# Stick-breaking attention with its heads cut into stages, projection blocks set between the stages in a fixed TensorE order, and the rotary tables computed during the first MLP

## Chip, core and metric

The kernel runs on one core of a Trainium2 chip. The metric is the device time of one execution in microseconds (us), as the median of several runs. Engine names in the profile: PE is TensorE (matmul), PEld its weight load, DVE is VectorE, ACT is ScalarE, POOL is GpSimd, SP is the engine that issues most DMAs.

## What is computed

Two transformer blocks over 512 tokens of width 1024, all in float32. The part that the change touches is the first half of block 1 and one small table of block 2:

```
h    = rmsnorm(x, g_pre_mix);  proj = h @ w_in           # pool input, q, k, v
z    = q @ k.T * scale                                   # 8 heads of 64, strictly causal
attn = where(mask, exp(log_sigmoid(z) + tail), 0)        # tail: sum of log(1-sigmoid(z)) to the right
o_sb = attn @ v
gates = sigmoid(h @ w_gate + b_gate)
merged = gates[:, :1024]*y_pool + gates[:, 1024:]*y_sb
x = x + rmsnorm(merged @ w_out);  x = x + rmsnorm(relu(..w_up)^2 @ w_down)   # block 1's MLP
cos, sin = rope_tables(positions)                        # used by the two layers of block 2
```

## The kernel before

Activations lie with features on partitions and the 512 tokens along the free axis. Every float32 product is made of three matmuls of rounded parts (`mm3`, L373 to L375): weight-high by activation-high and by activation-low, weight-low by activation-high. A projection of 128 output features (`proj`) is 8 such blocks, 24 matmuls of 512 columns. The weights come as units of 8 blocks in a fixed list (`weight_plan`); `prep` (L344 to L354) loads a unit by a DMA of SP, rounds it on ACT (`whi`, L352) and takes the rest on POOL (`wlo`, L353), three units ahead of use, with four buffers for each of the two parts.

Block 1 begins with the norm's split of x and its sum of squares, the values of all heads (96 matmuls), then `r`, the reciprocal root of the norm (`rsqrt`, L459 to L461 on DVE). Then follow q and k of the first pair of heads, a transposition of r to a column (`column`, eight small matmuls at L487 that read r), and the values' eviction with that column. `rope_tables` (L808 to L859) is called next: about 25 DVE instructions of 128x512 on tiles of the pool `xp`, a sine and four copies on ACT, one DMA of the positions.

The loop over four pairs of heads projects q and k of the next pair (`qk`), then runs `head` twice. A head has four handovers between TensorE and the two vector engines. TensorE writes the scores into three PSUM banks zC, zB, zA (12 matmuls, L577 to L579). For each bank ACT takes Abs (L584), Exp and Ln (L337), DVE a maximum and sum (L587), ACT the rounded part (L590), DVE the rest (L591). TensorE adds the sums to the right into the banks in the order zC, zB, zA (L597, L602). ACT takes Exp of each bank (L337) and the rounded part (L610), DVE the rest (L611), and TensorE multiplies by the values (8 matmuls, L615). Behind the two heads of a pair stand the projections of some gates (`EARLY`) and one of the pooled branch (`pool`). With the first pair the stage has 22 projections; 20 of them come behind the column.

Nobody writes down the order of the instructions: the program's calls are in this order, and a scheduler arranges each engine's queue by its own estimate of times, so that TensorE's queue mixes projections and steps of the heads. Each engine then runs its queue in order; a waiting instruction holds all behind it. PSUM has three banks `mm` for projections, one `av`, one `st` and the three of the scores.

Of the kernel before, what the change touches and what calls it, by code (L numbers as in the profile page):

```python
# [35 lines left out]
EARLY = ((), (0,), (1, 2), (3, 4))  # L36
# [20 lines left out]
LAG = 5  # L57
WHOLE = (slice(0, S),)
# [188 lines left out]
class Kern:  # L247
# [93 lines left out]

# [58 lines left out]
    def proj_halves(self, pool, tag, acts, n, done, finish):  # L400
        """The last n columns of outputs, by halves of the tokens: done(column, its half, tokens),
        and finish(tokens) after the last column of a half, behind the first products of the next."""
        w = [[self.take(ahead=AHEAD if j == 0 and k < UNIT else 2) for k in range(len(acts))] for j in range(n)]
        ready = None
        for cs in HALVES:
            for j in range(n):
                ps = pool.tile([P, S // 2], F32, name=tag)
                for k, a in enumerate(acts):
                    self.mm3(ps, w[j][k], [t[:, cs] for t in a], k == 0, k == len(acts) - 1)
                    if k == LAG and ready is not None:  # L410
                        finish(ready)
                        ready = None
                done(j, ps, cs)
            ready = cs
        finish(ready)

# [1 line left out]
    def split(self, pool, src, tags, scale=None, lo_eng=None):  # L418
        """src (times a per-partition scale) as two float32r parts."""
        hi, lo = (pool.tile([P, S], FR, name=t) for t in tags)  # L420
        self.split_into(hi, lo, src, scale, lo_eng)
        return hi, lo

    def split_into(self, hi, lo, src, scale=None, lo_eng=None):
        nc = self.nc
        if scale is None:
            nc.scalar.copy(out=hi, in_=src)  # L427
            (lo_eng or nc.vector).tensor_tensor(out=lo, in0=src, in1=hi.bitcast(F32), op=ALU.subtract)
# [5 lines left out]
    def sq_add(self, acc, src, first, eng=None):  # L434
        """acc += src^2."""
# [16 lines left out]
    def rsqrt(self, out, src, n):  # L452
        """out = (src / n + eps)^-1/2: exp(-ln / 2), and a Newton step on it."""
# [9 lines left out]
    def norm_in(self, pool, gname, l, produce=None, parts=WHOLE, on_pool=KT - 2):  # L463
        """The split of x*g, tile by tile, and what gives r = rsqrt(mean(x^2) + eps)."""
# [18 lines left out]
    def column(self, pool, pp, tag, row):  # L483
        """[128, 512] with equal partitions -> [128 tokens, 4 token tiles]."""
# [8 lines left out]
    def block1(self):  # L493
# [12 lines left out]
        atp = at.__enter__()  # L506
        pp_ = tc.tile_pool(name="pp1", bufs=1, space=PSUM, reuse_waits="tile")
# [10 lines left out]
        # constants of the stick-breaking attention  # L518
# [17 lines left out]
        # v, with tokens on partitions  # L536
# [9 lines left out]
        def qk(p):  # L546
            res = []
            q = self.proj(ppw, "mm", acts)
# [11 lines left out]
            k = self.proj(ppw, "mm", acts)  # L560
# [7 lines left out]
            return res  # L568
# [4 lines left out]
        def head(h, kk, qh, ql, o):  # L573
# [19 lines left out]
            for j in (3, 2, 1, 0):  # L593
# [9 lines left out]
            av = ptile("av")  # L603
            at_ = {}
            for b, n in (("zA", S), ("zB", 384), ("zC", S)):
                t = self.xp.tile([P, S], F32, name="x")[:, :n]
# [5 lines left out]
                at_[b] = (hi, lo)  # L612
            for j, (b, c0, q0, n) in enumerate(where):
                for i, part in enumerate(at_[b]):
                    mm(av[:, q0:S], lhsT=vst[j][:, h, :], rhs=part[:, c0 : c0 + n], start=j == 0 and i == 0, stop=j == 3 and i == 1)  # L615
# [6 lines left out]
        def pool(g):  # L622
            """Trailing means of window w minus the token itself."""
            w = WINDOWS[g]
            ps = self.proj(ppw, "mm", acts)
# [3 lines left out]
            while step < w:  # L629
                s2 = self.xp.tile([P, S], F32, name="x")  # L630
# [8 lines left out]
        heads = qk(0)  # L639
        rcol = self.column(atp, ppw, "st", r)  # L640
        vst = []
        for t in range(4):
            vt = atp.tile([P, SBH, P], FR, name="v", bufs=4)
            src = vps[t].rearrange("p (h d) -> p h d", d=SBD)
            A.activation(out=vt[:, :, 0:SBD], in_=src, func=AF.Identity, scale=rcol[:, t : t + 1], bias=0.0)
            V.scalar_tensor_tensor(out=vt[:, :, SBD:P], in0=src, scalar=rcol[:, t : t + 1], in1=vt[:, :, 0:SBD].bitcast(F32), op0=ALU.mult, op1=ALU.subtract)
            vst.append(vt)
        self.rope_tables()
        for p in range(4):
            now, heads = heads, qk(p + 1) if p < 3 else None  # L650
            o = atp.tile([P, S], F32, name="o", bufs=1)
            for e in range(2):
                head(2 * p + e, *now[e], o)
            oacts.append(self.split(brp, o, ("oh", "ol")))
            for i in EARLY[p]:
                for half in range(2):
                    ps = self.proj(ppw, "mm", acts)
# [16 lines left out]
        # pooled branch  # L674
# [7 lines left out]
        # gates and merge  # L682
# [25 lines left out]
        # output projection, norm, residual  # L708
# [33 lines left out]
        # MLP  # L742
# [5 lines left out]
        for c in range(nch):  # L748
            a = []
            pss = self.proj_outer(pp, "b", acts, FIRST1, HALVES) if c == 0 else []  # L750
            for f_ in range(CHUNK1):
# [4 lines left out]
                a.append(self.split(fp, ps, ("ah", "al")))  # L756
            if c < nch - 1:
# [50 lines left out]
    def rope_tables(self):  # L808
# [7 lines left out]
        t = lambda n: self.xp.tile([P, S], F32, name="x")  # L816
        pi = self.xp.tile([P, S], I32, name="x")
        nc.sync.dma_start(out=pi, in_=self.pos_d.broadcast_to((P, S)))
        a, d, hi, lo = t("ta"), t("td"), t("thi"), t("tlo")
# [9 lines left out]
        V.tensor_copy(out=a, in_=pi)  # L829
# [32 lines left out]
    def layer2(self, l, produce=None, after=None):  # L862
# [16 lines left out]
        # gated input of the convolution  # L879
# [20 lines left out]
        # shared rotary part of the keys  # L900
# [12 lines left out]
        # low-rank inputs of keys, values and queries  # L913
# [138 lines left out]
        # convolution: tile 0 and some taps of tile 3 off VectorE, the others on it  # L1052
# [47 lines left out]
        # layer norm over the convolution's channels, silu  # L1100
# [32 lines left out]
        # MLP  # L1133
# [38 lines left out]
    def final(self, pp, a):  # L1172
        """The last columns of the last layer, the norm, the output."""
# [62 lines left out]
```

## Time and profile before

| | |
|---|---|
| median of 3 runs | 1931.41 us (1929.58 to 1932.46) |
| the profiled execution, first to last instruction (span) | 1931.2 us; no other time is given for it |
| TensorE busy | 1850.6 us, 96% of the span |
| VectorE, ScalarE, GpSimd busy | 53%, 49%, 49% |
| mean granted TensorE clock | 0.983 of full |
| chain that ended last, by engine | PE 80%, DVE 14%, ACT 3% |

A share of busy time is a mean over stages. TensorE's time is the program's time nearly everywhere, so what a stage costs is read from where TensorE stands still in it (the list of waits), from the clock granted there, and from what the other engines do just before.

### The profile page before, as it was taken

What the parts mean: (1) busy time and instruction counts of PE and PEld (TensorE: products, weight loads), DVE (VectorE), ACT (ScalarE), POOL (GpSimd) and SP (SyncE); (2) the same over time, 40 slices, a digit from 0 to 9 for tenths busy, and PEclk for the clock granted to TensorE, in tenths of its full rate; (3) what the DMA queues carried; (4) which work ended last, traced back from release to release, by engine and by line L of the source; (5) the groups of instructions that cost most, each with busy time, mean ns of one, the idle gap of its engine ahead of it and who ended that gap; (6) DMA issues with size and microseconds to landing.
All of it is one profiled execution on the core that took longest, in us unless ns stands there. A gap on an engine that the chain in (4) does not pass through costs nothing.

```text
span 1931.2 us, 22032 instructions
## 1 busy us (share of the span) xinstructions
PE 1850.6 (96%) x8414; PEld 1502.6 (78%) x8414; DVE 1016.1 (53%) x1441; ACT 945.7 (49%) x1438; POOL 949.4 (49%) x510
## 2 busy tenths in 40 slices
PE   7999899899999998999899999999989899999997
PEld 5777788888888888766688888888766688888886
DVE  8656562731022118999565315532999666404533
ACT  4766553453233335678554324443768654314442
POOL 4223254464444455966454444455866464444442
PEclk9999999999999998999999999999999999999999
DMA  5111134133223222210233222333210123222221
GB/s 188 55 55 63 46 105 142 55 110 98 98 98 99 94 92 66 88 39 23 68 101 98 97 92 97 98 98 98 88 50 33 48 98 101 95 94 96 99 98 55
DMA packets 48649, 164.89 MB, mean 85 GB/s; under 512 B 5536, under 2 KB 7584, under 8 KB 48544
## 3 DMA queue, kind: packets, MB, share of 16 engines
q1 hardware_dynamic: 46304, 160.34, 25.1%
q10 hardware_dynamic: 2240, 3.15, 0.5%
q8 instruction: 66, 1.08, 0.2%
q14 instruction: 39, 0.32, 0.1%
HBM read 161.37 MB, written 2.10 MB: 85 GB/s over the span
## 4 chain that ended last, share of the span: by engine, by line
PE 80%; DVE 14%; ACT 3%; issue 1%; DMA 1%; SPq 0%; POOL 0%; DVEq 0%; ACTq 0%
PE b L374 21%; PE b L373 21%; PE b L375 21%; DVE cv L1067 3%; PE mm L373 2%; PE mm L374 2%; PE s L997 2%; PE mm L375 2%; PE t L1014 1%; ACT whi L352 1%; PE av L1019 1%; DVE x L591 1%; DVE acc L442 1%; PE av L1020 1%; DVE sq L460 1%
## 5 line engine op out<-in xcount | busy, mean ns | idle before, releaser
L353 POOL TENSOR_TENSOR wlo<-raw,whi 128x1024 fp32r<-128x1024 f32 x300 | 724.7, 2418 | 840.0 <-ACT whi L352 821.9
L352 ACT CAST whi<-raw 128x1024 fp32r<-128x1024 f32 (+1 forms) x302 | 313.6, 1040 | 522.8 <-PE b L374 419.3
L374 PE MATMUL b<-xl,whi 128*128 128x512 f32 (+1 forms) x1296 | 493.4, 381 | 3.6 <-DVE xl L431 3.6
L373 PE MATMUL b<-xh,whi 128*128 128x512 f32 (+1 forms) x1296 | 495.5, 383 | 0.0
L375 PE MATMUL b<-xh,wlo 128*128 128x512 f32 (+1 forms) x1296 | 493.2, 381 | 0.0
L374 PEld LDWEIGHTS b<-xl,whi 128*128 128x128 f32 x1296 | 246.5, 190 | 51.2 <-DVE xl L431 4.3
L373 PEld LDWEIGHTS b<-xh,whi 128*128 128x128 f32 x1296 | 246.1, 190 | 47.4 <-issue 1.7
L375 PEld LDWEIGHTS b<-xh,wlo 128*128 128x128 f32 x1296 | 246.5, 190 | 45.7
L373 PE MATMUL b<-ah,whi 128*128 128x512 f32 (+1 forms) x646 | 243.6, 377 | 0.0
L374 PE MATMUL b<-al,whi 128*128 128x512 f32 (+1 forms) x646 | 243.2, 377 | 0.0
L375 PE MATMUL b<-ah,wlo 128*128 128x512 f32 (+1 forms) x646 | 243.2, 376 | 0.0
L1079 POOL TENSOR_TENSOR cacc<-cacc,pd 128x510 f32<-128x510 f32 (+14 forms) x94 | 125.8, 1338 | 48.4 <-ACT pd L1077 44.5
L374 PEld LDWEIGHTS b<-al,whi 128*128 128x128 f32 x646 | 121.6, 188 | 22.3
L375 PEld LDWEIGHTS b<-ah,wlo 128*128 128x128 f32 x646 | 121.6, 188 | 22.3
L373 PEld LDWEIGHTS b<-ah,whi 128*128 128x128 f32 x646 | 121.6, 188 | 22.2
L1067 DVE SCALAR_TENSOR_TENSOR cv<-u,vec,cv 128x497 f32<-128x497 f32 (+13 forms) x146 | 108.0, 740 | 4.9 <-ACT cv L1057 2.9
L1141 DVE TENSOR_TENSOR b<-b,r 128x512 f32<-128x512 f32 x88 | 60.8, 697 | 94.5 <-PE b L375 93.1
L1165 DVE TENSOR_TENSOR x<-x,b 128x512 f32<-128x512 f32 x30 | 20.6, 687 | 161.2 <-PE b L375 161.2
L459 DVE SCALAR_TENSOR_TENSOR sq<-b,r 128x512 f32<-128x512 f32 x5 | 3.5, 691 | 143.4 <-ACT r L337 143.4
L427 ACT CAST ah<-cg 128x512 fp32r<-128x512 f32 x44 | 27.3, 620 | 95.2 <-DVE cg L1160 95.2
L373 PE MATMUL mm<-xh,whi 128*128 128x512 f32 x176 | 71.7, 408 | 0.0
L374 PE MATMUL mm<-xl,whi 128*128 128x512 f32 x176 | 70.8, 402 | 0.0
(421 smaller groups left out, 2934.4 us busy)
## 6 DMA issues: line engine op xcount, KB each, us to landing
raw<-w SPq DMA_DIRECT2D x295, 512.0 KB, 3.3
x<-xT SPq DMA_DIRECT2D x8, 256.0 KB, 6.3
x<-xT ACTq DMA_DIRECT2D x8, 256.0 KB, 4.6
raw<-w SPq DMA_DIRECT2D x7, 256.0 KB, 2.6
outT<-o ACTq DMA_DIRECT2D x4, 256.0 KB, 2.5
outT<-o SPq DMA_DIRECT2D x4, 256.0 KB, 2.6
vec<-vec SPq DMA_DIRECT2D x1, 363.0 KB, 6.9
x<-pos SPq DMA_DIRECT2D x1, 256.0 KB, 4.2
```

The source lines that it names most:

```text
L352: nc.scalar.copy(out=hi[:, cs], in_=raw[:, cs])
L353: (eng or nc.gpsimd).tensor_tensor(out=lo[:, cs], in0=raw[:, cs], in1=hi[:, cs].bitcast(F32), op=ALU.subtract)
L373: mm(ps, lhsT=wb[0], rhs=xb[0], start=start, stop=False, **kw)
L374: mm(ps, lhsT=wb[0], rhs=xb[1], start=False, stop=False, **kw)
L375: mm(ps, lhsT=wb[1], rhs=xb[0], start=False, stop=stop, **kw)
L427: nc.scalar.copy(out=hi, in_=src)
L442: (eng or nc.vector).tensor_tensor(out=acc, in0=acc, in1=sq, op=ALU.add)
L997: mm(s, lhsT=q[:, qb * P : (qb + 1) * P], rhs=k, start=True, stop=True)
L1067: V.scalar_tensor_tensor(out=acc[:, o], in0=us[i][:, u], scalar=self.v("w_dw_conv_2", l, i * CONV_K + k), in1=acc[:, o], op0=ALU.mult, op1 ...
L1079: G.tensor_tensor(out=acc[:, o], in0=acc[:, o], in1=pd, op=ALU.add)
L1141: V.tensor_tensor(out=ps, in0=ps, in1=r, op=ALU.mult)
L1165: V.tensor_tensor(out=self.x[m], in0=self.x[m], in1=ps, op=ALU.add)
```

## The change

The order of a head is cut into functions, and the projections become a generator that yields after each of their 8 blocks. The attention part is written inside a context that keeps TensorE's queue in the order of the calls; the other engines' queues are still arranged by the scheduler. `split_q` and `split_k` are the old `qk` without its projections. `FILL_FIRST` and `FILL` are counts of blocks (three matmuls each): 8 ahead of the first scores, then per head 6, 4, 4 and 5, which are 8 + 8 x 19 = 160 blocks, the 20 projections. The temporary tiles of the last Exp and of `pool` move from the eight buffers of `xp` to a pool `pt` of three. One gate pair moves to an earlier pair of heads. `rope_tables` is called after the first 16 feature tiles of block 1's MLP, behind the last DVE instruction of their split; its temporaries are the buffers `f` and `sq` of the norms and the tables themselves.

```diff
-EARLY = ((), (0,), (1, 2), (3, 4))
+EARLY = ((0,), (1,), (2,), (3, 4))
+FILL_FIRST = 8
+FILL = (6, 4, 4, 5)
...
+    def proj_steps(self, pool, tag, acts, done):
+        ps = pool.tile([P, S], F32, name=tag)
+        for k, a in enumerate(acts):
+            self.mm3(ps, self.take(), a, k == 0, k == len(acts) - 1)
+            if k == len(acts) - 1:
+                done(ps)
+            yield
...
+        pt_ = tc.tile_pool(name="pt", bufs=3, reuse_waits="tile")
...
-        heads = qk(0)
-        rcol = self.column(atp, ppw, "st", r)
...
-        self.rope_tables()
-        for p in range(4):
-            now, heads = heads, qk(p + 1) if p < 3 else None
-            o = atp.tile([P, S], F32, name="o", bufs=1)
-            for e in range(2):
-                head(2 * p + e, *now[e], o)
-            oacts.append(self.split(brp, o, ("oh", "ol")))
-            for i in EARLY[p]:
...
-            pooled.append(pool(p))
+            for p in range(4):
+                if p < 3:
+                    yield from self.proj_steps(ppw, "mm", acts, q_done(p + 1))
+                    yield from self.proj_steps(ppw, "mm", acts, k_done(p + 1))
+                for i in EARLY[p]:
+                    for half in range(2):
+                        yield from self.proj_steps(ppw, "mm", acts, gate_done(i, half))
+                yield from self.proj_steps(ppw, "mm", acts, lambda ps, g=p: pooled.append(pool(g, ps)))
...
+        with tc.manual_schedule(engines={mybir.EngineType.PE}):
+            queries[0] = split_q(self.proj(ppw, "mm", acts))
+            split_k(self.proj(ppw, "mm", acts), queries[0], heads[0])
+            rcol = self.column(atp, ppw, "st", r)
...
+            fill(FILL_FIRST)
+            now = scores(0, *heads[0][0])
+            for h in range(SBH):
+                if h % 2 == 0:
+                    o = atp.tile([P, S], F32, name="o", bufs=1)
+                fill(FILL[0])
+                sums(*now, (3, 2))
+                fill(FILL[1])
+                sums(*now, (1,))
+                fill(FILL[2])
+                sums(*now, (0,))
+                at_ = weigh(now[0])
+                fill(FILL[3] if h < SBH - 1 else 10**6)
+                if h < SBH - 1:
+                    now = scores(h + 1, *heads[(h + 1) // 2][(h + 1) % 2])
+                mix_values(h, at_, o)
...
+            if c == 0:
+                self.rope_tables(self.last_lo)
...
-        pi = self.xp.tile([P, S], I32, name="x")
+        pi = self.rp.tile([P, S], I32, name="f", bufs=1)
...
-        V.tensor_copy(out=a, in_=pi)
+        self.issue_behind(V.tensor_copy(out=a, in_=pi), behind)
```

The call that builds the program also gets `dynamic_dma_scratch_size=4096`, which leaves more on-chip memory for tiles; the rest of the diff removes comments.

How the queues move, at three places. First, VectorE's queue where the norm's `r` is made (L459 to L461 before, L472 to L474 in the changed kernel; `acc` is the sum of squares, `x` with L823 to L848 the rotary tables). Before, the first, the middle and the last rows of that stretch:

```order
L442 TENSOR_TENSOR acc<-acc,sq 128x512
L829 CAST x<-x 128x512
L830 TENSOR_SCALAR x<-x,cst 128x512
...
L847 TENSOR_TENSOR x<-x 128x512
L848 TENSOR_TENSOR x<-x 128x512
...
L459 SCALAR_TENSOR_TENSOR sq<-st,r 128x512
L827 SCALAR_TENSOR_TENSOR x<-x 128x512
L460 SCALAR_TENSOR_TENSOR sq<-sq,r 128x512
```

and now:

```order
L455 TENSOR_TENSOR acc<-acc,sq 128x512
L472 SCALAR_TENSOR_TENSOR sq<-st,r 128x512
L473 SCALAR_TENSOR_TENSOR sq<-sq,r 128x512
L474 SCALAR_TENSOR_TENSOR r<-sq,r 128x512
L562 SCALAR_TENSOR_TENSOR mm<-mm,r 128x512
```

Seventeen rows with the rotary tables, which stood between the sum of squares and the norm, are gone from here.

Second, TensorE at the first sums of the sixth head (heads are counted from 0, so this is head 5; zC is the first bank, `mm` the projections). Before:

```order
L374 MATMUL mm<-xl,whi 128x512
L597 MATMUL zC<-x,ntri 128x256
L375 MATMUL mm<-xh,wlo 128x512
L373 MATMUL mm<-xh,whi 128x512
L374 MATMUL mm<-xl,whi 128x512
L597 MATMUL zC<-x,ntri 128x256 x3
L602 MATMUL zC<-x,none 128x256 x2
L375 MATMUL mm<-xh,wlo 128x512
```

and now:

```order
L379 MATMUL mm<-xh,wlo 128x512
L614 MATMUL zC<-x,ntri 128x256 x4
L619 MATMUL zC<-x,none 128x256 x2
L377 MATMUL mm<-xh,whi 128x512
```

The sums now stand in one piece behind a fixed count of projection blocks, where before single projection matmuls lay between the part that reads ACT's result and the part that reads DVE's. ACT's queue for the same bank reads now (L568 and L569 split the second half of the next pair's q, L641 copies half of the head's output, L604 makes the part that the sums wait for):

```order
L568 CAST qh<-mm 64x512
L569 CAST qh<-mm 64x512
L598 ACTIVATE x<-zC 128x512
L641 COPY ot<-av 64x512
L341 ACTIVATE x<-x 128x512
L356 CAST whi<-raw 128x1024
L341 ACTIVATE x<-x 128x512
L604 CAST x<-x 128x512
```

which is the order it had before but for the place of the copy.

Third, ACT's queue in block 1's MLP, where the first down projection runs (`ff` is the copy of its result). Before:

```order
L352 CAST whi<-raw 128x1024 x2
L762 COPY ff<-b 128x512
L352 CAST whi<-raw 128x1024 x2
L762 COPY ff<-b 128x512
```

and now:

```order
L356 CAST whi<-raw 128x1024 x2
L827 COPY ff<-b 128x512
L356 CAST whi<-raw 128x1024
L341 ACTIVATE sq<-te 128x512
L337 ACT_TABLE_LOAD
L923 COPY tk<-sq 32x512
L924 COPY tk<-sq 32x512
...
L356 CAST whi<-raw 128x1024
L827 COPY ff<-b 128x512
```

The sine, a table load and four copies stand ahead of a weight cast here. TensorE's queue is the same as before, row for row, behind the last head.

## Rows read from the trace of the kernel before

**Rows 1.** Waits of TensorE, 42 to 236 us: us in total, times, longest

```profile
PE st L487 <- DVE r L461: 6.9, 1, 6.9
PE zC L597 <- DVE x L591: 4.2, 3, 1.7
PE av L615 <- DVE plzC L611: 3.5, 3, 1.5
PE zC L597 <- ACT x L590: 3.0, 3, 2.3
PE zB L597 <- DVE x L591: 1.8, 3, 0.8
PE zA L597 <- DVE x L591: 1.5, 1, 1.5
```

**Rows 2.** Timeline of VectorE: start, us, engine, line, out<-in, count, [idle <-releaser]

```profile
23.32 2.29 DVE L829 CAST x<-x 128x512 f32<-128x512 int32 x1 [0.24 <-DMA x<-pos]
...
46.42 0.68 DVE L459 SCALAR_TENSOR_TENSOR sq<-st,r 128x512 f32<-128x512 f32 x1
...
48.83 0.68 DVE L461 SCALAR_TENSOR_TENSOR r<-sq,r 128x512 f32<-128x512 f32 x1
```

**Rows 3.** Timeline of ScalarE around the norm and the sine

```profile
33.21 0.72 ACT L337 ACTIVATE r<-r,lna 128x512 f32<-128x512 f32 x1
...
53.32 1.28 ACT L333 ACT_TABLE_LOAD   x1
54.62 0.58 ACT L555 CAST qh<-mm 64x512 fp32r<-64x512 f32 x1
```

**Rows 4.** Timeline of TensorE around the column of r

```profile
36.38 0.39 PE L373 MATMUL mm<-xh,whi 128*128 128x512 f32 x1
...
42.27 0.39 PE L375 MATMUL mm<-xh,wlo 128*128 128x512 f32 x1
49.56 1.87 PE L487 MATMUL st<-e,r 128*128 128x1 f32 x8 [6.90 <-DVE r L461]
51.29 0.77 PE L373 MATMUL mm<-xh,whi 128*128 128x512 f32 x1
...
57.31 0.40 PE L375 MATMUL mm<-xh,wlo 128*128 128x512 f32 x1
```

**Rows 5.** Windows: us, busy (x) of PE PEld DVE ACT POOL, PEclk, DMA share, GB/s

```profile
51.29:235.12 183.83, 169.90 (x801) 136.94 (x802) 111.60 (x150) 126.56 (x214) 50.86 (x26) 0.97 0.17 56
100.00:120.00 20.00, 18.37 (x86) 14.88 (x85) 12.32 (x18) 13.88 (x24) 5.36 (x3) 0.91 0.15 52
180.00:200.00 20.00, 17.74 (x81) 14.15 (x80) 13.10 (x17) 10.96 (x19) 6.87 (x6) 0.93 0.16 52
```

**Rows 6.** Timeline of VectorE: subtractions L591 of three heads, last split of the MLP

```profile
71.94 0.69 DVE L591 TENSOR_TENSOR x<-x 128x512 fp32r<-128x512 f32 x1 [0.68 <-ACT x L590]
...
112.36 2.45 DVE L591 TENSOR_TENSOR x<-x 128x512 fp32r<-128x512 f32 x1 [0.73 <-ACT x L590]
...
174.38 1.08 DVE L591 TENSOR_TENSOR x<-x 128x512 fp32r<-128x512 f32 x1 [0.69 <-ACT x L590]
...
460.22 0.69 DVE L428 TENSOR_TENSOR al<-b,ah 128x512 fp32r<-128x512 f32 x1 [0.65 <-ACT ah L427]
```

**Rows 7.** Groups by line and form, GpSimd, 60 to 236 us: xcount | busy us, mean ns

```profile
L353 POOL TENSOR_TENSOR wlo<-raw,whi 128x1024 fp32r<-128x1024 f32 x19 | 46.4, 2441 | 124.8 <-ACT whi L352 124.7
```

**Rows 8.** Timeline of ScalarE: two heads, the norm after block 1's mixing, the MLP

```profile
68.60 0.60 ACT L584 ACTIVATE x<-zC 128x512 f32<-128x512 f32 x1
...
168.54 0.58 ACT L555 CAST qh<-mm 64x512 fp32r<-64x512 f32 x1 [0.74 <-PE zC L577]
...
370.21 0.42 ACT L441 ACTIVATE sq<-x 128x256 f32<-128x256 f32 x1 [0.45 <-POOL acc L442]
...
473.61 1.05 ACT L352 CAST whi<-raw 128x1024 fp32r<-128x1024 f32 x1 [3.91 <-issue]
...
479.05 1.05 ACT L352 CAST whi<-raw 128x1024 fp32r<-128x1024 f32 x1 [4.39 <-PE b L374]
```

More of the change, by code (lines that the diff above doesn't have):

```diff
@@ L427, in split_into @@
             nc.scalar.copy(out=hi, in_=src)
-            (lo_eng or nc.vector).tensor_tensor(out=lo, in0=src, in1=hi.bitcast(F32), op=ALU.subtract)
+            self.last_lo = (lo_eng or nc.vector).tensor_tensor(out=lo, in0=src, in1=hi.bitcast(F32), op=ALU.subtract)
         else:
@@ L506, in block1 @@
         atp = at.__enter__()
+        pt_ = tc.tile_pool(name="pt", bufs=3, reuse_waits="tile")
+        pt = pt_.__enter__()
         pp_ = tc.tile_pool(name="pp1", bufs=1, space=PSUM, reuse_waits="tile")
@@ L545, in block1, with split_q @@
         r = fin(ppw, "st")
-        def qk(p):
-            res = []
-            q = self.proj(ppw, "mm", acts)
+        def split_q(q):
             V.scalar_tensor_tensor(out=q, in0=q, scalar=SBD**-0.5, in1=r, op0=ALU.mult, op1=ALU.mult)
@@ L559, in qk, with split_k @@
                 qs.append((qh, ql))
-            k = self.proj(ppw, "mm", acts)
+            return qs
+        def split_k(k, qs, res):
             V.tensor_tensor(out=k, in0=k, in1=r, op=ALU.mult)
@@ L567, in qk, with scores @@
                 res.append((kk,) + qs[e])
-            return res
         where = [("zA", 0, 0, S), ("zB", 0, P, 384), ("zC", 0, 256, 256), ("zC", 256, 256, 256)]
-        def head(h, kk, qh, ql, o):
+        def scores(h, kk, qh, ql):
             banks = {b: ptile(b) for b in ("zA", "zB", "zC")}
@@ L592, in head, with sums @@
                 sp[b] = (hi, lo)
-            for j in (3, 2, 1, 0):
+            return banks, sp
+        def sums(banks, sp, js):
+            for j in js:
                 b, c0, q0, n = where[j]
@@ L602, in head, with weigh @@
                         mm(z[:, d0 : d0 + n2], lhsT=none, rhs=part[:, c2 : c2 + n2], start=False, stop=j2 == 3 and i == 1, skip_group_check=True)
-            av = ptile("av")
+        def weigh(banks):
             at_ = {}
             for b, n in (("zA", S), ("zB", 384), ("zC", S)):
-                t = self.xp.tile([P, S], F32, name="x")[:, :n]
+                t = pt.tile([P, S], F32, name="pt")[:, :n]
                 self.act(AF.Exp, out=t, in_=banks[b][:, :n])
@@ L612, in head, with mix_values @@
                 at_[b] = (hi, lo)
+            return at_
+        def mix_values(h, at_, o):
+            av = ptile("av")
             for j, (b, c0, q0, n) in enumerate(where):
@@ L620, in head, with pool @@
             V.tensor_tensor(out=o[me], in0=av[me], in1=t[me], op=ALU.add)
-        def pool(g):
+        def pool(g, ps):
             w = WINDOWS[g]
-            ps = self.proj(ppw, "mm", acts)
             u = zgp.tile([P, S], F32, name="z")
@@ L629, in pool @@
             while step < w:
-                s2 = self.xp.tile([P, S], F32, name="x")
+                s2 = pt.tile([P, S], F32, name="pt")
                 V.tensor_tensor(out=s2[:, step:], in0=s[:, step:], in1=s[:, : S - step], op=ALU.add)
@@ L638, in block1, with fill_steps, q_done, k_done @@
         oacts, zgate, pooled = [], {}, []
-        heads = qk(0)
-        rcol = self.column(atp, ppw, "st", r)
[L641 to L647, printed above, removed]
-        self.rope_tables()
-        for p in range(4):
-            now, heads = heads, qk(p + 1) if p < 3 else None
-            o = atp.tile([P, S], F32, name="o", bufs=1)
-            for e in range(2):
-                head(2 * p + e, *now[e], o)
-            oacts.append(self.split(brp, o, ("oh", "ol")))
-            for i in EARLY[p]:
-                for half in range(2):
-                    ps = self.proj(ppw, "mm", acts)
+        heads = [[] for _ in range(4)]
+        queries = [None] * 4
+        def fill_steps():
+            def q_done(p):
+                return lambda ps: queries.__setitem__(p, split_q(ps))
+            def k_done(p):
+                return lambda ps: split_k(ps, queries[p], heads[p])
+            def gate_done(i, half):
+                def done(ps):
                     z = zgp.tile([P, S], F32, name="z")
@@ L660, in block1, with fill @@
                     zgate[i, half] = z
-            pooled.append(pool(p))
+                return done
+            for p in range(4):
[6 more added lines that the diff above has]
+                yield from self.proj_steps(ppw, "mm", acts, lambda ps, g=p: pooled.append(pool(g, ps)))
+        filling = fill_steps()
+        def fill(n):
+            for _ in range(n):
+                next(filling, None)
+        with tc.manual_schedule(engines={mybir.EngineType.PE}):
+            queries[0] = split_q(self.proj(ppw, "mm", acts))
+            split_k(self.proj(ppw, "mm", acts), queries[0], heads[0])
+            rcol = self.column(atp, ppw, "st", r)
+            vst = []
+            for t in range(4):
+                vt = atp.tile([P, SBH, P], FR, name="v", bufs=4)
+                src = vps[t].rearrange("p (h d) -> p h d", d=SBD)
+                A.activation(out=vt[:, :, 0:SBD], in_=src, func=AF.Identity, scale=rcol[:, t : t + 1], bias=0.0)
+                V.scalar_tensor_tensor(out=vt[:, :, SBD:P], in0=src, scalar=rcol[:, t : t + 1], in1=vt[:, :, 0:SBD].bitcast(F32), op0=ALU.mult, op1=ALU.subtract)
+                vst.append(vt)
+            fill(FILL_FIRST)
[14 more added lines that the diff above has]
+                mix_values(h, at_, o)
+                if h % 2:
+                    oacts.append(self.split(brp, o, ("oh", "ol")))
+        self._close(pt_)
         self._close(at)
@@ L805, in _close, with rope_tables @@
         cm.__exit__(None, None, None)
-    def rope_tables(self):
+    def rope_tables(self, behind):
         tc, nc = self.tc, self.nc
@@ L815, in rope_tables @@
         c3 = two_pi - c1 - c2
-        t = lambda n: self.xp.tile([P, S], F32, name="x")
-        pi = self.xp.tile([P, S], I32, name="x")
+        pi = self.rp.tile([P, S], I32, name="f", bufs=1)
         nc.sync.dma_start(out=pi, in_=self.pos_d.broadcast_to((P, S)))
-        a, d, hi, lo = t("ta"), t("td"), t("thi"), t("tlo")
+        a, d = (self.rp.tile([P, S], F32, name="sq") for _ in range(2))
+        hi, lo = te, tk
         fr, ph, pl = (self.cst[:, i : i + 1] for i in range(3))
@@ L1228 @@
     arr = arrays(inputs)
[L1229 removed]
+    nc = bacc.Bacc("TRN2", target_bir_lowering=False, num_devices=1, dynamic_dma_scratch_size=4096)
     args = [nc.dram_tensor(n, a.shape, mybir.dt.from_np(a.dtype), kind="ExternalInput").ap() for n, a in arr.items()]
```

1 line of the change is left out of this document (removed).

## The prediction

> **What bounds the kernel now.** I read the page's shares first: TensorE is busy nearly all the time, so a change pays only where TensorE stands still or runs at a low clock. Then the list of TensorE's waits for the stage that is changed [rows 1]. The longest, 6.9 us, is the column of r (L487), which waits for VectorE's last step of r; the five others, 14.0 us together, are the handovers inside the heads. The timeline of VectorE shows why r is late: the rotary tables begin at 23.32, and the first step of r (L459) comes at 46.42, the last ends at 49.51 [rows 2], although ScalarE had the exponential that it needs at 33.93 [rows 3]. VectorE works through the tables in between, because they stand ahead in its queue. TensorE's timeline shows the price [rows 4]: the projections run one per 0.2267 us (26 steps from 36.38 to 42.27), end at 42.50, and the next 512-column matmul begins at 51.29.
>
> The window from there to the end of the attention part is 183.83 us [rows 5]. It holds 480 projection matmuls of 512 columns, and eight heads of 40 matmuls with 12,800 columns (scores 3,840, sums 6,144, values 2,816): 348,160 columns. At 0.2267 us per 512 that is 154.2 us; 29.6 us are loss. 14.0 of them are the waits above. The clock takes 6.0: from 51.29 to 57.31 TensorE issues 14 matmuls in 6.02 us where 3.17 do at the full clock [rows 4], so 2.85; the slices with a mean clock of 0.91 and 0.93 [rows 5] hold 18% and 14% of 20 us at the lower of the two levels (1.2 against 2.4 GHz), half of it lost, 1.8 and 1.4. The other 9.6 us are short steps: matmuls of fewer columns and the start of each handover.
>
> **The change, part by part.**
>
> *Rotary tables out of the start.* 26 VectorE instructions leave the stretch between the sum of squares and r; the sine, its two table loads, four copies and one DMA leave ScalarE's and SP's queues there. r then follows the exponential: 33.93 and three steps of 0.68 [rows 2, 3] make 36.0, ahead of the last k matmul at 42.50. The column no longer waits; its own 1.73 us (49.56 to 51.29) stay. TensorE's next work there, the scores of head 0, needs the values' banks emptied. VectorE and ScalarE have 24 matmuls (5.4 us) behind the column for eight instructions of 0.6 to 0.75, so I cost that at nothing; if it were not covered, it would cost 1 to 2 us. Gain 7.1 us: 49.56 becomes 42.5.
>
> *The fixed order.* Columns and matmuls are the same, 154.2 us, and I keep the 9.6 us of short steps. What changes is where TensorE waits. The two vector engines' time from scores to the first sums has three measured cases. A clean one begins with Abs at 68.60 [rows 8] and ends with the subtraction at 72.63 [rows 6]: 4.03 us. One with two q casts, a copy and a weight cast in front or between begins at 168.54 [rows 8] and ends at 175.46 [rows 6]: 6.92 us, and head 5 of the changed kernel has the same eight ScalarE instructions. In the third a subtraction of 0.69 takes 2.45 (112.36) [rows 6], as long as one GpSimd weight split of 2.44 [rows 7] that had begun before. The cover is fixed now: eight value matmuls and 18 projection matmuls, 12,032 columns, 5.3 us (4.1 for head 0, with no values ahead); 3.4 to 3.5 us more for each of the next two sums; 6.0 us from the last sums to the last value part. TensorE cannot take another block while it waits.
>
> I went through ScalarE's new queue head by head with these durations, placing a GpSimd split of 2.44 behind each weight cast. Late by: head 0 1.1 (q casts, small cover), 0.3 and 0.5; head 1 0.3; head 2 0.6 and 1.0 (weight cast ahead of the rounded part); head 3 0.3, 1.1 and 0.6; head 4 nothing; head 5 6.9 - 5.3 = 1.6, and 0.6 at the values (weight cast ahead of the last part); head 6 2.0 (a weight cast between zB's Ln and its rounding, then the held subtraction); head 7 1.5 (a table load ahead of the last part). Sum 11.5 us, against 14.0 now. Below it could be 5 (only heads 5, 6 and 7 late, as 4.03 us elsewhere are covered); above, 22 (six more subtractions held by 2.45 - 0.69 = 1.76). I take 11.5, between the clean and the held rows, since both occur.
>
> *Clock.* The fall after the long wait goes with it. Of the 13 waits inside the old heads [rows 1] two were followed by a slice with a lower clock [rows 5]. The new list has about as many, but none as long as the 2.3 of rows 1, so I take one fall, 1.5 us (0 to 4.3).
>
> *The table load in head 7.* The load back to another set lasts 1.28 us, and the next ScalarE instruction starts at 54.62, 0.02 behind its end [rows 3]; that is the duration in the list. The Trainium skill, "ScalarE: Activation LUTs", "What ACT_TABLE_LOAD costs", counts 1.28 for the load and 1.38 for a drain at each switch; no row here shows a drain, and by the page head 7 would be late by 2.9 and the sum 1.4 us longer, 1918.4.
>
> *Tables in the MLP.* They start behind the last split, at 460.91 [rows 6], in a stretch where VectorE has nothing else. Before, they lasted from 23.32 to beyond 49.51 between GpSimd's splits [rows 2], say 28 us; 26 at 0.69 would be 18. So ScalarE, which gets to the sine at 474.66 [rows 8], may wait until 479 to 489, and the sine, load and copies take 4.4 us more. Behind them waits a weight cast, now at 479.05: it would be 4 to 14 us late. A unit is cast three units of 5.44 us (473.61 to 479.05) before use, less 1.05 and 2.44 for cast and split: 12.8 us of cover. Cost 0, at most 1.5; nothing, because with the casts held GpSimd has no split to do and the tables speed up. The positions' DMA stands on SP behind a wait for the old `f`, but the next weight DMA there waits later, for GpSimd. A table load moves in front of the squares at 370.21, where ScalarE idles 0.45 and VectorE leads: 0 to 1.3, I take 0.
>
> *Smaller moves.* Three `pt` buffers shared by Exp and the pooled branch: 0, at most 2.4 for each of three heads. One `mm` bank is held longer by a q: before too, 0. The descriptor memory and the gates' other place: 0.
>
> *Sum.* The new window is 154.2 + 9.6 + 11.5 + 1.5 = 176.8 us, 7.0 less than 183.8. 1931.2 - 7.1 - 7.0 = 1917.1 us against the profiled span, for which no other time is given; the median is 0.2 above it. I say 1917.
>
> **Rivals.** *The fixed order covers nearly all.* Lateness 5, no clock fall, half of the 9.6 us gone because the two parts of a sum follow each other: a window of 164, and 1931.2 - 7.1 - 19.8 = 1904. For it: 4.03 us fits under 5.3 everywhere. Against: weight casts in six heads.
>
> *Only the early removal pays.* The scheduler's order already put free matmuls into the gaps; the new one is late by 20 and the clock falls twice: 154.2 + 9.6 + 20 + 3 = 186.8, which is 3.0 more than now, and 1931.2 - 7.1 + 3.0 = 1927. For it: TensorE has nothing to step to. Against: head 4's and 1's chains fit.
>
> *Nothing in sum*, 1931: the same with a lateness of 24, or the third rival with a stall of 4 us in the MLP because the sine waits beyond the cover. The tables would have to last over 32 us there, against 28 in the busiest stretch of the trace.
>
> *Slower: the clock falls in every head.* Each head has one or more short waits now at a fixed place. If each brought TensorE to 1.2 GHz as the wait at 49.56 did, 2.85 us a head, eight heads cost 22.8 instead of 1.5: 1917.1 + 21.3 = 1938. It decides from seven such falls on. Against it: eleven of the 13 old waits left the clock alone. The Trainium skill, "TensorE: Matmul & The Clock Gate", "A second HAM failure mode: psum-queue depth-cycling", says that frequent short idles between groups of matmuls make the clock go to and fro; by that rule this would be the outcome, and the trace bears it out in two of 13 cases.
>
> **Numbers.** Forecast (1911 to 1923) 0.56; covered nearly all 0.20; only the early part 0.13; nothing 0.06; slower 0.05. About 0.2%, 3.9 us, can be told from no change. Of the third case, 1927, about half lies under 1927.5. So faster 0.56 + 0.20 + 0.07 = 0.83, same 0.06 + 0.06 = 0.12, slower 0.05. The range reaches from the well-covered case to the third, 1904 to 1928.
>
> **What would show it.** No wait at the column, and r done near 36; the first scores begin near 50; the attention part ends near 221 rather than 235; waits of TensorE inside the heads of 8 to 16 us, most of them for a subtraction, heads 5 and 6 among them, head 4 without; one or two low-clock slices there. In the MLP TensorE does not wait though ScalarE waits for the tables. I am wrong if the column still waits, if the heads' waits pass 20 us or stay under 5, if the clock falls in most heads, or if anything behind 236 us differs by over 2 us.

## The result and the profile after

The changed kernel takes 1911.18 us (median of 4 runs, 1910.96 to 1911.9), beside 1931.93 us for the kernel before: a ratio of 0.9893, 95% interval 0.9879 to 0.9907. The profiled execution has a span of 1909.4 us against 1931.2, so 21.8 us less. The forecast was 1917, within 1904 to 1928: sign and places were right, and the gain in the heads was underrated.

TensorE's timeline around the column of r, which answers to [rows 4] (start, us, engine, line, operation, out<-in):

```profile
42.11 0.39 PE L379 MATMUL mm<-xh,wlo 128*128 128x512 f32 x1
42.34 0.95 PE L500 MATMUL st<-e,r 128*128 128x1 f32 x8
43.15 0.49 PE L377 MATMUL mm<-xh,whi 128*128 128x512 f32 x1
...
48.73 0.39 PE L591 MATMUL zA<-qh,kk 128*128 128x512 f32 x1
...
212.57 0.39 PE L377 MATMUL b<-xh,whi 128*128 128x512 f32 x1
```

The column follows its predecessor without a wait and lasts 0.81 us to the next start instead of 1.73. The attention part ends at 212.57 instead of 235.12, 22.55 us earlier. VectorE's steps of r, to be read beside [rows 2]:

```profile
33.98 0.69 DVE L472 SCALAR_TENSOR_TENSOR sq<-st,r 128x512 f32<-128x512 f32 x1 [11.09 <-ACT r L341]
34.71 1.96 DVE L473 SCALAR_TENSOR_TENSOR sq<-sq,r 128x512 f32<-128x512 f32 x1
36.70 0.69 DVE L474 SCALAR_TENSOR_TENSOR r<-sq,r 128x512 f32<-128x512 f32 x1
```

VectorE now waits for the exponential, and r is done at 37.39, five microseconds ahead of the column. TensorE's waits from 40 to 214 us answer to [rows 1] (total, times, longest, in us):

```profile
PE zB L614 <- DVE x L605: 2.7, 2, 1.6
PE zC L614 <- DVE x L605: 2.7, 4, 1.2
PE av L637 <- DVE plzC L629: 1.1, 2, 0.7
PE zC L614 <- ACT x L604: 0.5, 2, 0.3
PE zA L614 <- ACT x L604: 0.4, 1, 0.4
PE zA L614 <- DVE x L605: 0.3, 1, 0.3
PE av L637 <- ACT phzC L628: 0.2, 1, 0.2
```

They sum to 7.9 us, where it was 14.0. The window that answers to the first of [rows 5] shows the full clock throughout (0.97 before):

```profile
43.15:212.57 169.42, 161.21 (x802) 134.50 (x802) 104.72 (x143) 117.41 (x200) 53.01 (x29) 1.00 0.18 61
```

169.42 less 154.2 for the columns and 7.9 of waits leaves 7.3 us of short steps (9.6 before). In the MLP the sine came at 458.79, after ScalarE had waited 6.36 us for the tables, and a weight cast stood behind it:

```profile
458.79 0.63 ACT L341 ACTIVATE sq<-te 128x512 f32<-128x512 f32 x1 [6.36 <-DVE te L919]
459.44 1.28 ACT L337 ACT_TABLE_LOAD   x1
...
463.26 1.05 ACT L356 CAST whi<-raw 128x1024 fp32r<-128x1024 f32 x1
```

Casts come every 5.44 us there, so this one was due at 456.82. It is late by 6.4 us, and TensorE has no wait from 349 to 600 us: nobody feels it.

### The profile page after: what moved, and what is told of

The parts are those of the page before. It is cut to its first block, busy times and chain, and to the rows that moved or that the text cites. A ratio compares the mean times of both kernels' runs of the same rounds, so it can differ in the third digit from the quotient of the medians.

```text
span 1909.4 us, 22035 instructions
## 1 busy us (share of the span) xinstructions
PE 1841.1 (96%) x8414; PEld 1499.3 (79%) x8414; DVE 1008.6 (53%) x1441; ACT 946.1 (50%) x1438; POOL 948.7 (50%) x510
## 3 DMA queue, kind: packets, MB, share of 16 engines
q8 instruction: 66, 1.08, 0.2%
## 4 chain that ended last, share of the span: by engine, by line
PE 83%; DVE 11%; ACT 3%; issue 1%; DMA 0%; POOL 0%; DVEq 0%; ACTq 0%; SPq 0%; POOLq 0%
PE b L378 21%; PE b L379 21%; PE b L377 21%; DVE cv L1132 3%; PE mm L377 3%; PE mm L378 3%; PE mm L379 3%; PE s L1062 3%; PE t L1079 1%; PE av L1084 1%; ACT whi L356 1%; PE av L1085 1%; DVE acc L455 1%; DVE sq L473 1%; DVE x L605 1%
## 5 line engine op out<-in xcount | busy, mean ns | idle before, releaser
L455 POOL TENSOR_TENSOR acc<-acc,sq 128x256 f32<-128x256 f32 (+1 forms) x49 | 55.3, 1129 | 31.3 <-ACT sq L454 29.9
L818 DVE TENSOR_TENSOR b<-rl,b 128x512 f32<-128x512 f32 x32 | 22.1, 696 | 90.1 <-ACT rl L817 90.1
```

What stands on the lines that cost most here:

```text
L455: (eng or nc.vector).tensor_tensor(out=acc, in0=acc, in1=sq, op=ALU.add)
L818: V.tensor_tensor(out=ps, in0=rl, in1=ps, op=ALU.mult)
```

## The experiments

Ratios are to the kernel before on the same chip. "Window" is the time from the first projection behind the column to the end of the attention part, and "waits" are TensorE's in it. Both are read from one profiled execution of each run, which lay between 4.0 us below (e11) and 2.3 us above (e3) the run's median.

| run | median us | ratio, 95% | window us | waits us |
|---|---|---|---|---|
| before | 1931.93 | 1 | 183.83 | 14.0 |
| changed | 1911.18 | 0.9893 (0.9879 to 0.9907) | 169.42 | 7.9 |
| e1 tables only | 1922.47 | 0.9943 (0.9926 to 0.996) | 178.97 | 14.6 |
| e2 order only | 1926.1 | 0.9965 (0.9952 to 0.9979) | 176.17 | 10.5 |
| e3 order left to the scheduler | 1914.05 | 0.9898 (0.9882 to 0.9915) | 172.11 | 9.4 |
| e4 19, 0, 0, 0 | 1920.07 | 0.9929 (0.991 to 0.9949) | 175.24 | 13.3 |
| e5 no weight split | 1905.35 | 0.9854 (0.9832 to 0.9876) | 161.32 | 2.1 |
| e6 17, 0, 0, 2 | 1907.88 | 0.9872 (0.9853 to 0.9891) | 164.53 | 4.7 |
| e7 9, 4, 4, 2 | 1912.17 | 0.9892 (0.9873 to 0.991) | 169.82 | 6.4 |
| e8 changed again | 1910.63 | 0.9885 (0.9866 to 0.9903) | 169.39 | 7.9 |
| e9 casts behind the chains | 1904.75 | 0.9843 (0.9829 to 0.9858) | 163.44 | 4.2 |
| e10 the same, 17, 0, 0, 2 | 1911.76 | 0.9884 (0.9868 to 0.9901) | 166.44 | 6.6 |
| e11 the same, 15, 0, 0, 4 | 1905.11 | 0.9842 (0.9827 to 0.9856) | 159.33 | 1.8 |

### The two parts apart (e1, e2)

e1 is the kernel before with `rope_tables` in the first MLP; e2 is the changed kernel with it back ahead of the heads.

```diff
 e1: kernel before
-        self.rope_tables()
...
+            if c == 0:
+                self.rope_tables(self.last_lo)
 e2: changed kernel
+            self.rope_tables()
             fill(FILL_FIRST)
...
-            if c == 0:
-                self.rope_tables(self.last_lo)
```

> The kernel before with one edit: the rotary tables are computed in the first MLP, as in the changed kernel. TensorE's queue is row for row that of the kernel before. Theory (the start and the order of the heads pay apart, and add up): the column of r no longer waits for the tables (7.2 us), takes 0.8 instead of 1.7 us (0.9), and the stretch at the lower clock behind it is gone (2.9): about 1931.9 - 11.0 = 1921, with the heads' waits near 14 us as before. Rival A (TensorE arrives at the heads earlier but the two vector engines do not, so that the gain is given back as new waits in the first heads): 1925 to 1931. Rival B (the tables were all of it, the order of the heads pays nothing): 1911.

> The changed kernel with one edit undone: the rotary tables stand again where they were, ahead of r. TensorE's queue is row for row that of the changed kernel. Theory (the two parts add up): the column waits 6 to 7 us again, 2.9 us go at the lower clock behind it, and the heads' waits stay at 8 us without a fall of the clock: 1911.2 + 11.0 = 1922. Rival B (the order pays nothing): 1931. Rival C (the late r is covered by the eight blocks ahead of the first scores, and only the order paid): 1911 to 1915.

e1 gave 0.9943, 1922.5 us where the theory had 1921. Its attention part ends at 222.33 us, 12.8 us earlier than before, and that of the changed kernel another 9.8 us earlier. The 9.8 us lie between two windows at the full clock. They belong to all that e1 lacks: the order in stages, and with it the gates' other place and the `pt` buffers, which no run takes apart. The waits of e1 in the heads are nearly those of the kernel before:

```profile
PE zC L597 <- DVE x L591: 4.2, 3, 1.7
PE av L615 <- DVE plzC L611: 3.4, 3, 1.5
PE zC L597 <- ACT x L590: 3.0, 3, 2.3
PE zB L597 <- DVE x L591: 2.5, 3, 1.6
PE zA L597 <- DVE x L591: 1.5, 1, 1.5
```

yet its window has a mean clock of 1.00:

```profile
43.36:222.33 178.97, 164.30 (x802) 132.43 (x802) 108.22 (x144) 119.33 (x204) 50.89 (x26) 1.00 0.18 58
```

The two low-clock slices of [rows 5], 3.2 us by the prediction, are gone with the waits unchanged. So 3.2 of the 12.8 us can't be put down to the tables. By the medians the tables give 9.9 of 20.8 us.

e2 gave 1926 instead of 1922. The theory had left out a cost, seen in TensorE's waits of e2:

```profile
PE st L500 <- DVE r L474: 6.9, 1, 6.9
...
PE zA L591 <- DVE v L704: 2.1, 1, 2.1
...
PE zC L591 <- DVE v L704: 0.8, 1, 0.8
```

r is late, and ScalarE has the sine, a table load and four copies (53.19 to 58.82) ahead of the values' eviction. The eight blocks ahead of the first scores no longer cover it: 2.9 us. With these waits comes a stretch at the lower clock (0.91 from 60 to 80 us), some 1.8 us more. e2's attention part ends 7.1 us earlier than before; with e1's 12.8 that is 19.9, and 2.6 are missing to 22.55. The uncovered wait is of that size. But the slower stretches inside the heads differ too (two before, one in e2, none in e1 and the changed kernel), so it is likely, and not shown, that each part helps the other a little.

### Is it the kept order? (e3)

```diff
-        with tc.manual_schedule(engines={mybir.EngineType.PE}):
+        if True:
```

> The changed kernel without the context that keeps TensorE's queue in the order of the calls; the calls in single blocks stay. The scheduler then moves a few dozen of TensorE's rows and cuts the sums apart again. Theory (what pays is that the calls come in stages with blocks between them, not that the order is kept): 1909 to 1913, with more changes of bank and so a few tenths of short steps more. Rival D (keeping the order is what pays, the scheduler's estimate of times puts the sums too early again): 1917 to 1925, waits in the heads of 14 us or more.

0.9898 cannot be told from the changed kernel's 0.9893 and 0.9885. The profile has a window 2.7 us longer, with 1.5 us more of waits and one stretch at the lower clock. So what pays lies in the calls, in stages with single blocks between them (e4 changes only where the blocks stand); that the order is then kept is worth little, if anything.

### How much cover, and where (e4, e6, e7, and e8 as their level)

```diff
-FILL = (6, 4, 4, 5)
+FILL = (19, 0, 0, 0)                              # e4
+FILL = 7 * ((17, 0, 0, 2),) + ((13, 0, 0, 6),)    # e6, one row per head
+FILL = 7 * ((9, 4, 4, 2),) + ((7, 3, 3, 6),)      # e7
```

> The changed kernel with the 19 blocks of a head in one piece ahead of its sums (19, 0, 0, 0) instead of (6, 4, 4, 5). The sums then have 12.9 us of cover and do not wait; behind the last sum stand only the next scores (1.7 us), so that scores and values wait for three exponentials, three casts and the subtractions, about 5 us. Theory (a wait costs its length, the clock mostly stays): about 3 us a head, 24 us: 1930 to 1940. Rival E (a wait of this length brings the clock down in every head, as the column's did): 2.9 us a head more, 1950 to 1960. Rival F (the cut into stages does not matter, the total of blocks does): 1911.

All three theories of e4 missed: 0.9929. The sums do not wait, and the scores of seven heads wait only 1.3 us each, the values in the last head alone:

```profile
PE zA L591 <- ACT pt L341: 5.3, 7, 1.2
PE av L637 <- ACT phzA L628: 3.8, 1, 3.8
PE zC L591 <- ACT pt L341: 3.7, 7, 0.7
PE av L637 <- DVE plzA L629: 0.5, 1, 0.5
```

I had put all three exponentials, casts and subtractions on the path (3 us a head), but the scores and the values' first parts run beside them. Some 2.4 of the 3.8 us are no matter of cover: zA's sums were done at 210.89, but ScalarE's first exponential of that head began at 213.34, behind GpSimd, for a buffer that e7 shows below. Sixteen waits brought one stretch at the lower clock, behind the one of 3.8 us. A fall in every head, the rival on the slower side, is refuted for waits of this size.

> The changed kernel with 17 blocks ahead of all sums of a head and 2 behind them (13 and 6 in the last head). In the run with 19 in one piece the last bank's subtraction was done 1.1 to 4.7 us ahead of its sum, and what waited were the next scores, about 1.3 us a head, and the last values, 3.8 us. Theory (cover can be pooled: a head's three chains need about 11 to 12 us in all, the exponentials need two blocks): waits in the heads at most 3 us, 1903 to 1906. Rival H (the scores wait for the exponentials whatever stands ahead of them, since those begin behind the last sum): 8 to 10 us of waits again, 1911 to 1914.

> The changed kernel with (9, 4, 4, 2) blocks a head, (7, 3, 3, 6) in the last, instead of (6, 4, 4, 5). Theory (the first sums had too little cover and the values three blocks too much): the waits for zC go (3.3 us), those of zB and zA too (3.5 us), values and scores wait under 2 us in all: 1902 to 1905. Rival H: the scores wait for the exponentials, 0.5 to 1.3 us a head: 1908 to 1912.

> The changed kernel itself, beside the runs above on the same chip: 1909 to 1913, waits of 8 us in the heads. It gives the level for runs that differ from it by a few us.

e8 sets the level, 0.9885. e6 gave 1907.9 (0.9872), 2.8 us under e8's median: its sums wait 0.2 us in all. By its window, 4.9 us less, the theory holds in direction; it had 1903 to 1906, and the intervals overlap. e7's theory missed. Its sums wait 0.2 us too, and its waits are 1.5 us shorter than the changed kernel's, but its window is no shorter:

```profile
43.40:213.22 169.82, 162.97 (x802) 137.32 (x802) 105.77 (x142) 117.65 (x200) 51.85 (x28) 0.98 0.18 61
```

The mean clock of 0.98 hides two stretches at the lower level, 0.53 from 110.30 to 113.90 and 0.51 from 171.80 to 175.30, at most 3.4 us lost; the changed kernel has none in its window. So e7 does not tell whether its rows of blocks are better or worse. Its longest wait, 2.5 us for zA's next scores, goes back to the exponential that stands behind GpSimd (ScalarE's timeline of e7):

```profile
166.00 1.05 ACT L356 CAST whi<-raw 128x1024 fp32r<-128x1024 f32 x1 [2.32 <-PE mm L378]
170.63 0.60 ACT L341 ACTIVATE pt<-zA 128x512 f32<-128x512 f32 x1 [3.57 <-POOL pt L653]
```

That is the buffer `pt` that the exponentials share with the pooled branch. With five blocks behind the sums this is hidden, with two it is not; e6 shows the same at 165.90 (3.84 us of idle). In the third head (head 2) both runs wait 2.1 us for the values, because a weight cast and two q casts came between an exponential and its rounded part (ScalarE's timeline of e6):

```profile
105.64 0.61 ACT L341 ACTIVATE pt<-zC 128x512 f32<-128x512 f32 x1
106.13 1.06 ACT L356 CAST whi<-raw 128x1024 fp32r<-128x1024 f32 x1
107.21 0.58 ACT L568 CAST qh<-mm 64x512 fp32r<-64x512 f32 x1
107.80 0.58 ACT L569 CAST qh<-mm 64x512 fp32r<-64x512 f32 x1
108.29 0.62 ACT L628 CAST phzC<-pt 128x512 fp32r<-128x512 f32 x1
```

### What makes the sums late (e5, e9)

In the changed kernel the seventh head (head 6) shows both suspects at once, on ScalarE, GpSimd and VectorE:

```profile
178.79 1.04 ACT L356 CAST whi<-raw 128x1024 fp32r<-128x1024 f32 x1
179.74 0.50 ACT L604 CAST x<-x 128x384 fp32r<-128x384 f32 x1
...
179.91 2.39 POOL L357 TENSOR_TENSOR wlo<-raw,whi 128x1024 fp32r<-128x1024 f32 x1 [5.11 <-ACT whi L356]
...
178.92 0.56 DVE L601 SCALAR_TENSOR_TENSOR x<-zB,x 128x384 f32<-128x384 f32 x1 [0.29 <-ACT x L341]
...
180.27 2.44 DVE L605 TENSOR_TENSOR x<-x 128x384 fp32r<-128x384 f32 x1 [0.20 <-ACT x L604]
```

A weight cast stands ahead of the rounded part and sets off a weight split. The cast itself costs the chain only 0.3 us, since VectorE's step ahead of the rounded part (L601, 178.92 and 0.56 us) ended at 179.48. The subtraction begins 0.36 us behind the start of the split and ends 0.41 us behind its end, after 2.44 us instead of 0.56. e5 leaves the splits out, so that its low-part matmuls read the high part; e9 keeps the casts out of the chains:

```diff
 e5
-            (eng or nc.gpsimd).tensor_tensor(out=lo[:, cs], ...)
+            if not self.no_lo:
+                (eng or nc.gpsimd).tensor_tensor(out=lo[:, cs], ...)
 e9
-            nc.scalar.copy(out=hi[:, cs], in_=raw[:, cs])
+            cast = nc.scalar.copy(out=hi[:, cs], in_=raw[:, cs])
+            if self.gate is not None:
+                self.issue_behind(cast, self.gate)
...
-                A.copy(out=hi, in_=t)
+                self.gate = A.copy(out=hi, in_=t)     # in scores and in weigh
```

> The changed kernel with GpSimd's weight splits left out for the units that are prepared in the attention part: their low-part matmuls read the high part instead, so that part of the products is not computed; TensorE's and ScalarE's numbers of instructions stay. Theory (half of the waits that are left come from subtractions of VectorE that stand behind a weight split of GpSimd): no subtraction lasts over 1.1 us, the waits in the heads fall from 8 to 3 to 4 us, 1911 - 5 = 1906. Rival G (the waits come from ScalarE's order, weight casts ahead of the rounded parts): subtractions become short but the waits stay at 7 to 8 us: 1911.

> The changed kernel with (6, 4, 4, 5) kept, and with one more rule for ScalarE's queue: a weight cast that is called for after a head's scores stands behind the last of the three rounded parts, one called for after its exponentials behind the last of those. Theory (what makes a handover late is a weight cast in the chain, or a subtraction behind the GpSimd split that the cast sets off; the cover of (6, 4, 4, 5) is enough for the bare chain): waits in the heads 2 to 4 us instead of 8, no first sum later than 0.7 us, 1903 to 1907. Rival K (the splits only move, on to the subtractions ahead of the values, and the chain is short of cover by itself): 6 to 9 us, 1909 to 1912. Rival L (casts held back come too late for TensorE's projections): waits of projections for weights.

The groups of the subtraction, changed kernel, e5 and e9 (shortest, median, longest in ns):

```profile
L605 DVE TENSOR_TENSOR x<-x x24: 557/693/2517, 55.0 to 203.2; 128x512 fp32r<-128x512 f32 x16, 128x384 fp32r<-128x384 f32 x8
```
```profile
L607 DVE TENSOR_TENSOR x<-x x24: 540/692/694, 55.5 to 195.4; 128x512 fp32r<-128x512 f32 x16, 128x384 fp32r<-128x384 f32 x8
```
```profile
L608 DVE TENSOR_TENSOR x<-x x24: 540/692/693, 54.8 to 196.0; 128x512 fp32r<-128x512 f32 x16, 128x384 fp32r<-128x384 f32 x8
```

In e5 seven of the 24 chains still have a weight cast inside (eight in the changed kernel, by ScalarE's timelines), and the waits are 2.1 us. So it is the held subtraction, not the cast, that cost the larger part of the 7.9 us. ScalarE's queue differs in a few other places in e5, which this run does not separate. e9 gets the same short subtractions through ScalarE's queue: a cast behind the chain starts its split behind the chain. Its waits fall to 4.2 us. No projection waits for a weight. What is left are mostly first sums (2.0 us) and the last values:

```profile
PE av L640 <- DVE plzC L632: 1.8, 2, 1.1
PE zC L617 <- ACT x L607: 1.0, 2, 0.7
PE zC L617 <- DVE x L608: 1.0, 3, 0.4
```

### A version that beats both (e10, e11)

Both use e9's rule; (17, 0, 0, 2) and (15, 0, 0, 4) are their rows of blocks, 13 and 6, 12 and 7 in the last head.

> The same rule for ScalarE's queue with 17 blocks ahead of all sums and 2 behind. Theory (both remedies act on the same waits, so they do not add fully): waits at most 3 us, those for the exponentials and the last values, no fall of the clock in the heads: 1902 to 1905. Rival K: two splits in a row now fall on the exponentials' subtractions, the values wait 1 us or more in most heads: 1908 to 1912.

> The same rule with 15 blocks ahead and 4 behind (12 and 7 in the last head). Theory (a bare chain needs 10 to 11 us and the 15 blocks with the values of the head before give 11.4): like the run with 17 and 2 within 2 us, 1902 to 1906, with waits for the exponentials gone. Rival M (15 blocks are too few for the chain): a wait of 1 to 2 us for zA in most heads, 1910 to 1916.

e9 and e11 are faster than the changed kernel, 0.984 against 0.9893, with intervals that do not meet. e11's window of 159.33 us is 5.1 above the columns' 154.2; its one wait is

```profile
PE av L640 <- DVE plzB L632: 1.8, 1, 1.8
```

in the first head, where the casts held back cause three splits just ahead of the values. e10 shows that two blocks behind the sums are too few: the scores wait 4.5 us for exponentials, in the pooled heads again for `pt`. More `pt` buffers were not tried.

### The cover in the MLP (e12)

```diff
+                self.rope_tables(self.last_lo)
                 self.rope_tables(self.last_lo)
```

> The changed kernel with the rotary tables computed twice over in the first MLP (the second time with the same result). In the changed kernel the first sine came at 458.8 us, a weight cast was held 6.4 us and no projection waited. Theory (a unit's cast has 12.8 us of cover, so one set of tables is free with some 6 us to spare, and a second set that holds the next cast by 11 to 16 us uses it up): a wait of TensorE of 0 to 5 us there, nothing elsewhere: 1911 to 1916. Rival N (VectorE's and ScalarE's queues are free enough for any amount there): no wait, 1911. Rival O (the first set was not free, only hidden in the numbers behind it): more than 8 us.

The execution took 1913.4 us. The second sine came at 479.33, after 14.72 us in which ScalarE stood still, and TensorE had one wait there:

```profile
PE b L379 <- POOL wlo L357: 1.7, 1, 1.7
```

One set of tables is free there, a second one costs 1.7 us in this one execution: the cover ends between the two, which fits the 12.8 us of the prediction.

## Why the prediction was right, and where its sizes were off

The forecast said that the end of the attention part would come 14.1 us earlier; it came 22.55 us earlier. By its own steps:

- **Column of r, 7.1 us.** Measured 7.2 (49.56 to 42.34). Right, and e2 brings the wait back at the same 6.9 us. r was done at 37.39 and not at 36.0, since L473 took 1.96 us; the column did not feel it. The column's own 1.73 us I kept; it took 0.81, since before it had run behind an idle TensorE at the lower clock (0.50 from 49.56 to 51.29). Missed, 0.9.
- **Eviction of the values, nothing.** Right in the changed kernel. The price if uncovered, given as 1 to 2 us, is 2.9 in e2.
- **Lateness, 11.5 us.** Measured 7.9. By head, forecast and measured: 1.9 and 1.0; 0.3 and 0; 1.6 and 2.0; 2.0 and 1.6; 0 and 0; 2.2 and 1.0; 2.0 and 1.5; 1.5 and 0.9. The list found the right heads, and head 6 is late in the way worked out (cast between Ln and rounding, then the held subtraction), but most entries were high. In head 3 a wait at one handover is cover for the next, and I had added them as if it were not: the wait of 1.6 us for zB leaves the part for zA 1.8 us early. In head 5 the chain took 6.91 us (151.03 to 157.94), as forecast, but TensorE waited only 1.0 for it and not at the values; why this and the other entries were high, the runs do not take apart.
- **Clock, one fall, 1.5 us.** None came. All I had was that two of 13 waits were followed by a slower slice. e1 has the same TensorE queue, the same waits within 0.7 us and no slower slice, while e3 with 11 waits has one and e7 with seven has two. So the number of waits does not give this term, and the one fall was a guess. The Trainium skill, "TensorE: Matmul & The Clock Gate", "A second HAM failure mode: psum-queue depth-cycling", has the clock go to and fro with frequent short idles; the changed kernel's 13 short waits left it at 1.00.
- **Short steps, 9.6 us kept.** This was the other mis-sized step: 7.3 are left. TensorE changed between projections and steps of the heads 146 times in the window before and 65 times now. By the steps from one matmul's start to the next, the changes without a wait cost 2.7 us beyond their columns in e1, which has the old queue at the full clock, and 0.4 now: that is the size of the difference. A dozen of them in e1 cost some 0.11 us each. The first rival had this, as "half of the 9.6".
- **Table load ahead of the last part, 1.5 us.** 0.9. The load lasts 1.28, and the next cast starts 0.02 behind its end (209.03, 210.33), again no drain.
- **Tables in the MLP, 0; smaller moves, 0.** Right; the tables lasted from 438.60 to 459.88, 21 us of the 18 to 28. The `pt` buffers cost nothing with five blocks behind the sums; in e7 they cost up to 2.5 us, the size of the bound. Behind the attention part the gain shrinks from 22.55 to 21.8 us, within the 2 us allowed; the lower clock behind the norm lasted longer there than before (0.50 from 339.00 to 349.30, against 0.51 from 364.30 to 371.30).

Sum of the misses at the end of the attention part: 3.6 (lateness), 2.3 (short steps), 1.5 (clock), 0.9 (column), 0.2 (its start), 8.5 in all; less 0.75 given back later, 7.7, which is 1917.1 less 1909.4. The truth lies between the forecast and its first rival, and both had the mechanism. Three slips in the working moved nothing: 1917.1 and a drain of 1.38 are 1918.5, not 1918.4; a stall of 4 us in the MLP needs tables of 30.5 us, not over 32 (460.91 + 30.5 + 4.4 is 16.8 behind 479.05, of which 12.8 are covered); and of the 26 instructions of the tables 22 stood ahead of r.

## What to carry to other kernels

Where a chain of two vector engines feeds TensorE in stages, give TensorE a counted number of independent blocks between the stages, and count a chain's cover over the whole stage rather than per handover. Then look at what else starts in the chain: here a weight cast put on ScalarE at the wrong place set off a GpSimd split that held VectorE's subtraction, and moving the casts behind the chain shortened the heads by another 6 us, beside the 9.8 us of their new order. Work that only needs to be early enough, like the tables, belongs where its engine idles, with the first weight behind it counted.

## What the runs showed of the hardware

VectorE's subtraction with both inputs in SBUF is held by a GpSimd split that began before it, also for 0.56 us of work (2.44 us above). The six of L605 that began inside a split in the changed kernel ended 0.41 to 0.56 us behind the split's end. Four of them lasted 1.08 to 2.52 us; the other two began in its last 0.4 us. Two subtractions of L629 that began 0.09 us ahead of a split (130.95 and 170.46) kept their 0.68 us, and the splits took 2.86 and 2.87 us instead of 2.40. The step that reads scores from PSUM was never held, though seven began inside a split:

```profile
L601 DVE SCALAR_TENSOR_TENSOR x<-zC,x x8: 684/692/692, 53.6 to 194.9; 128x512 f32<-128x512 f32 x8
```

The Trainium skill, "SBUF — State Buffer", "Who interferes with whom", says that a VectorE instruction with two inputs in SBUF contends with a GpSimd instruction that reads SBUF and that one with at most one does not, outside the two-port modes. These rows agree.

The other surprise is the clock: the same list of waits, 14 us against 14.6, on a TensorE queue that is the same row for row, came with two slower slices in the kernel before and with none in e1. Nor does a shorter list spare them: e7, with seven waits and 6.4 us, has two. The length of a wait alone did not tell which it would be.
